# Dilated attention in an S5 hybrid layer: queries and values loaded a step ahead, V from three buffers, and the turned P kept in P's own tile

## The chip, the cores and the metric

The kernel runs on one core of a Trainium2 chip, in one launch. The metric is device time in microseconds (us), from one execution of the whole program. Before the change it is 2058.14 us, the median of three runs from 2056.48 to 2062.57. Engines are named as the profile names them: PE is the matrix engine (PEld its weight loads), DVE the vector engine, ACT the scalar engine, POOL GpSimd, and SP the engine that here only issues DMAs.

## The reference

One encoder layer on 2048 tokens of width 1024. An S5 state-space branch (32 groups of 16 channels, both directions) and an attention branch read the same normalised input; each is gated and projected, the two are mixed by sigmoid gates, and an output projection is added to the input.

```python
h = rms_norm(x, norm_w); proj = h @ w_in
u_a, z_a, q, k, v, z_b, g = split(proj)
for p, (window, dilation) in enumerate(((128, 1), (512, 4), (2048, 16))):
    o, lse = dilated_band_attention(q[:, :, p], k, v, window, dilation)   # 8 heads of 64
    # s = q k^T / 8, masked to the band; p = exp(s - max); o = (p v) / sum(p); lse = max + log(sum)
attn = sum over p of softmax(lse)[p] * o[p]
y_b = (attn * silu(z_b)) @ w_proj_attn
y_s = gelu(bidir_s5(u_a, ...));  a, b = split(y_s @ w_glu + b_glu)
y_a = (a * sigmoid(b) * silu(z_a)) @ w_proj_ssm
out = x + (sigmoid(g_a) * y_a + sigmoid(g_b) * y_b) @ w_out
```

Everything is float32. The kernel keeps that by splitting an operand into a high and a low part and taking three matmuls for one (`mm3`).

## The kernel before

The program has three phases. Phase A (to about 1083 us of the profiled span) makes the projections and the state-space part, and leaves Q, K and V in HBM. Phase B (to about 1670) is the attention. Phase C is the two branch projections, the mix and the output projection.

**Attention.** `attn_steps` lists 80 steps: four pairs of heads (hp), in each of them the three patterns in the order p = 1, 0, 2, in each of them four quarters of the queries (quad). A quarter with p 1 or 0 is two steps of two query tiles, with p 2 one step of four. The steps that share a quarter are a group, of which there are 48. A step j has three parts, and they are written one step apart: in turn i of the loop stand the scores of step i, the turning of step i-1 and the values of step i-2.

- `attn_scores`: in the first step of a group it issues the loads of q (two tiles, pool `qa`, two buffers) and v (one tile of five 128-row pieces, pool `vp`, two buffers). PE then multiplies q by K into two PSUM tiles `s` (of three); DVE's reduction (L1010) adds the mask, finds the row minimum and writes the masked scores to P in SBUF; ACT takes the exponential in place (L1014). P is two pairs of tiles `p00, p10` and `p01, p11`, one pair a step in turn.
- `attn_turn`: PE transposes the eight 128x128 blocks of P into two PSUM tiles `pp`; ACT (L1030) and DVE (L1032) each copy one of them to SBUF tiles `t0` and `t1`, which have two buffers each.
- `attn_values`: PE multiplies T by v into `po`, and at the end of a group it is copied out.

POOL issues the loads of q and v, but for the first two groups, which SP issues. With p = 1 the five pieces of v are five DMAs (L978): two edges of 64 rows, whose other half POOL sets to zero, and three whole pieces.

**Side work.** After each part, `self.run` lets PE do a share of other work: the remaining projections, the gated linear unit (`glu`), and the first part of the branch projection (`mix_early`). In `glu`, four results `fth` a block of tokens are made by ACT (L1189) and DVE (L1190, L1191) and stored to ACTA by SP (L1192); the next block's input is prepared in two halves `ft` (L1151 to L1156). `fth` and `ft` share two buffers of one pool (`ev`, tag e1), so the second half of `ft` waits until the store of the `fth` before it has landed. Matmuls of the side work write `acc`, of which there are two. `attn_merge` joins the three patterns of a quarter on POOL and DVE, through loads `ab` of weights that were stored to AL a moment before.

**What sets the order.** The program is written in the order of the loop, and is then put in order by the tile framework's scheduler (`schedule_with_timeline_sim=True`). That gives each engine one fixed list of instructions with semaphore waits. On the chip an engine works through its list in order; an instruction that waits holds everything behind it on the same engine.

Of the kernel before, what the change touches and what calls it, by code (L numbers as in the profile page):

```python
# [9 lines left out]
F32 = mybir.dt.float32  # L10
F32R = mybir.dt.float32r
# [14 lines left out]
def f(ap):  # L26
    return ap.bitcast(F32)


def at(t, off, dims):  # L30

    return bass.AP(tensor=t.tensor, offset=t.offset + off, ap=dims)
# [7 lines left out]
class Kern:  # L40
# [862 lines left out]
    def attn_setup(self, base, ctx, pctx):  # L903
        ap, R = self.pool, dict(ctx=ctx, side="right")
        self.op = ap("op", ctx=base, side="right")
        self.kp = ap("kp", **R)
        self.qa = ap("qa", bufs=2, **R)
        self.vp = ap("vp", bufs=2, **R)
        self.aw = ap("aw", bufs=2, **R)
        mp = ap("mk", **R)  # L910
        self.mg = ap("mg", **R)

        self.kh = [self.kp.tile([128, 2048], F32R, name=f"kh{h}") for h in range(2)]
        self.kl = [self.kp.tile([128, 2048], F32R, name=f"kl{h}") for h in range(2)]
        self.mk = {}
        for n in ("m2", "m1", "m3"):
            t = mp.tile(list(self.ins[n].shape), F32, name=n)
            self.nc.sync.dma_start(t, self.ins[n])
            self.mk[n] = t
        self.pS = ap("pS", bufs=3, space=PSUM, ctx=pctx)  # L920
        self.pT = ap("pT", bufs=2, space=PSUM, ctx=pctx)
        self.pO = ap("pO", bufs=1, space=PSUM, ctx=pctx)
        self.ev_ = 0
        self.P = [[self.aw.tile([128, 512], F32, name=f"p{h}{i}", bufs=1) for h in range(2)] for i in range(2)]
        for t in self.P[0] + self.P[1]:
            self.nc.vector.memset(t, 0.0)
        self.turn_ = 0
        self.O = [self.op.tile([128, 2048], F32, name=f"o{p}", tag=f"o{p}") for p in range(2)] + [None]

# [8 lines left out]
    def attn_steps(self):  # L938
# [12 lines left out]
            prev = x["group"]  # L951
        return out

    def attn_scores(self, x):
        nc, mm, R, C = self.nc, self.mm, 2048, 512
        hp, p, quad, per, g = x["hp"], x["p"], x["quad"], x["per"], x["group"]
        tiles = self.tiles[p]
        if x["sub"] == 0:
            late = hp > 0 or p != 1 or quad > 1

            g["q"] = [self.qa.tile([128, 512], F32R, name=f"q{h}") for h in range(2)]
            for h in range(2):
                o = (8 * p + 2 * hp + h) * 2 * 64 * R + 512 * quad
                (nc.gpsimd if late else nc.sync).dma_start(f(g["q"][h]), at(self.QT, o, [[R, 128], [1, 512]]))

            v = g["v"] = self.vp.tile([128, 5, 128], F32, name="v")
            c0 = 128 * hp
            if p == 2:
                (nc.gpsimd if late else nc.sync).dma_start(v[:, :4], at(self.V, 512 * quad * C + c0, [[4 * C, 128], [C, 4], [1, 128]]))
            else:  # L970
                run = 8 if p == 0 else 32
                base, m0 = (0, 4 * quad) if p == 0 else (512 * quad, 0)
                for m in range(m0, m0 + 5):
                    j0, j1 = max(run * m - run // 2, 0), min(run * m + run // 2, 128)
                    if j1 - j0 < run:
                        nc.gpsimd.memset(v[64:, m - m0], 0.0)
                    rows = [[512 * C, 4], [C, 4 * (j1 - j0)]] if p == 0 else [[C, 4 * (j1 - j0)]]
                    (nc.gpsimd if late else nc.sync).dma_start(v[:(16 if p == 0 else 4) * (j1 - j0), m - m0],  # L978
                                                               at(self.V, (base + 4 * j0) * C + c0, rows + [[1, 128]]))
            if p == 2:  # L980
                self.st[2] = self.aw.tile([128, 2, 2, 4], F32, name="st2", bufs=3)
            elif quad == 0:
                self.st[p] = self.aw.tile([128, 2, 2, 16], F32, name="st")
        q, kh, kl = g["q"], self.kh, self.kl
        st = x["st"] = self.st[p]
        w = 512 // per
        S = [self.pS.tile([128, per, w], F32, name="s") for h in range(2)]
        self.turn_ += 1
        x["P"] = [t.rearrange("p (i w) -> p i w", i=per) for t in self.P[self.turn_ % 2]]
        for i, t in enumerate(x["idx"]):  # L990
            qs = slice(128 * (t % 4), 128 * (t % 4) + 128)
            for h in range(2):
# [6 lines left out]
        for h in range(2):  # L999
            for i, t in enumerate(x["idx"]):  # L1000
                nk, mask = tiles[t][2], self.mk[tiles[t][1]]
                c = (t, 4 * (t % 4) + t // 4, t % 4)[p]
                least, o = st[:, 0, h, c:c + 1], 0
# [13 lines left out]
    def attn_turn(self, x):  # L1017

        nc, tiles = self.nc, self.tiles[x["p"]]
        x["blocks"] = blocks = [(i, b, b * tiles[t][3][0][1], vt, n) for i, t in enumerate(x["idx"])  # L1020
                                for b, (vt, n) in enumerate(tiles[t][3])]
        x["T"] = []
        for h in range(2):
            pp = self.pT.tile([128, 4, 128], F32, name="pp")
            for c, (i, b, o, vt, n) in enumerate(blocks):
                self.tr(pp[:, c], x["P"][h][:, i, o:o + 128], self.ident)
            ts = self.aw.tile([128, 4, 128], F32, name=f"t{h}")
            self.ev_ += 1
            if self.ev_ % 2:
                nc.scalar.activation(ts, pp, AF.Copy)  # L1030
            else:
                nc.vector.tensor_copy(ts, pp)  # L1032
            x["T"].append(ts)

    def attn_values(self, x):
        nc, mm, R = self.nc, self.mm, 2048
# [261 lines left out]
    def phase_b(self, base):  # L1298
        ctx, pctx = ExitStack(), ExitStack()
        self.attn_setup(base, ctx, pctx)  # L1300
        self.tiles = [self.q_tiles(p) for p in range(3)]
        self.st = [None] * 3
        steps = self.attn_steps()
        n = len(steps)
        self.beside, self.credit, self.since = self.fill(), 0.0, 0.0
        for r in range(4):
            self.k_load(0, r)
        self.run(LEAD)
        self.merges = []
        for i in range(n + 2):  # L1310
            self.merges = [m for m in self.merges if next(m, self) is not self]
            for d, fn in enumerate((self.attn_scores, self.attn_turn, self.attn_values)):
                j = i - d
                if 0 <= j < n:
                    x = steps[j]
                    fn(x)
                    if d == 0 and x["p"] == 2 and x["hp"] < 3:
                        self.k_load(x["hp"] + 1, x["quad"])
                    self.run(PACE[self.part] * (P2 if steps[min(i, n - 1)]["p"] == 2 else 1.0))
        if self.part == 2:  # L1320
            self.marks = {}
        for _ in range(4):
            self.run(TAIL)
            self.merges = [m for m in self.merges if next(m, self) is not self]
        pctx.close()
        ctx.close()
        self.run(1e9)
        self.flush()
# [169 lines left out]
```

## Time and profile before

| | |
|---|---|
| median of three runs | 2058.14 us |
| the profiled execution | 2057.8 us, its span 2056.0 us |
| PE busy, over the span | 1960.6 us (95%) |
| DVE, POOL, ACT busy | 1283.1, 838.7, 722.2 us |
| mean granted clock of PE | 0.978 of full speed |
| DMA engines' time for POOL's queue (q, v and K loads), for SP's | 8.2%, 42.3% |

The profile is of one execution. The 1.8 us between its time and its span lie outside what the instructions show. A busy share says how long an engine worked, not whether its work decided the end; for that one reads which waits PE has, and where.

### The profile page before, as it was taken

How to read it: one execution, taken by the hardware profiler on the slowest of the kernel's cores; microseconds unless marked ns; L12 is line 12 of the kernel's file. 1: busy time of each engine (PE TensorE's matmuls, PEld its weight loads, DVE VectorE, ACT ScalarE, POOL GpSimd, SP SyncE). 2: the span in 40 equal slices, each digit the busy share in tenths (PEclk: the TensorE clock that was granted, in tenths of full speed). 3: DMA queues.
4: the chain of work that ended last, by engine and by line, in shares of the span. 5: the costliest groups of instructions: out<-in, count | busy, mean ns of one | idle time of the engine just before them, and what ended most of it. 6: DMA issues, size and time to landing. Idle time of an engine off the chain costs nothing.

```text
span 2056.0 us, 37526 instructions
## 1 busy us (share of the span) xinstructions
PE 1960.6 (95%) x13612; PEld 1762.9 (86%) x13612; DVE 1283.1 (62%) x3276; ACT 722.2 (35%) x1789; POOL 838.7 (41%) x1128
## 2 busy tenths in 40 slices
PE   6899999999999999899998999999998978999999
PEld 6788899999787889899987878878887978899997
DVE  8867584878657688577765445456677656333332
ACT  4221242333222233233325545445665623101110
POOL 4410465548645755375543347457355232000000
PEclk9999999999999999999999999999999989999999
DMA  6632465346533454634465476567777447433332
GB/s 195 196 99 74 129 194 150 111 122 172 166 113 109 132 174 123 183 111 134 132 210 167 130 207 179 176 179 209 232 186 202 133 144 238 133 118 114 113 113 77
DMA packets 272059, 312.55 MB, mean 152 GB/s; under 512 B 86594, under 2 KB 182226, under 8 KB 271874
## 3 DMA queue, kind: packets, MB, share of 16 engines
q1 hardware_dynamic: 250914, 260.39, 42.3%
q0 software_dynamic: 20960, 49.76, 8.2%
q8 instruction: 108, 1.77, 0.4%
q14 instruction: 77, 0.63, 0.1%
HBM read 202.12 MB, written 105.71 MB: 150 GB/s over the span
## 4 chain that ended last, share of the span: by engine, by line
PE 62%; DVE 15%; DMA 12%; SPq 3%; POOL 3%; issue 3%; ACT 2%; DVEq 0%; POOLq 0%; ACTq 0%
PE acc L53 42%; PE po L53 11%; PE s L53 3%; PE pp L56 3%; DVE wlo L311 2%; DMA ab<-AL 2%; DMA raw<-in_w_in 1%; DMA ACTA<-fth 1%; DMA raw<-in_w_out 1%; PE y L53 1%; DMA AL<-e 1%; DVE zs L843 1%; DMA ST<-sr 1%; PE tp L56 1%; DVE zs L841 1%
## 5 line engine op out<-in xcount | busy, mean ns | idle before, releaser
L53 PE MATMUL acc<-xh,whi 128*128 128x512 f32 (+1 forms) x960 | 376.4, 393 | 18.1 <-DVE xsc L379 8.7
L53 PE MATMUL acc<-whi,xh 128*128 128x256 f32 x1280 | 368.3, 288 | 4.6 <-ACT qr L451 3.6
L53 PE MATMUL acc<-xl,whi 128*128 128x512 f32 (+1 forms) x960 | 366.5, 382 | 1.1 <-DVE xl L208 1.1
L53 PE MATMUL acc<-xh,wlo 128*128 128x512 f32 (+1 forms) x960 | 365.1, 381 | 0.0
L53 PE MATMUL acc<-whi,xl 128*128 128x256 f32 x1280 | 364.5, 285 | 0.4 <-POOL xl L263 0.4
L53 PE MATMUL acc<-wlo,xh 128*128 128x256 f32 x1280 | 364.6, 285 | 0.0
L53 PEld LDWEIGHTS acc<-whi,xh 128*128 128x128 f32 x1280 | 247.7, 194 | 7.7 <-ACT qr L451 4.2
L53 PEld LDWEIGHTS acc<-whi,xl 128*128 128x128 f32 x1280 | 247.7, 194 | 0.8 <-POOL xl L263 0.6
L53 PEld LDWEIGHTS acc<-wlo,xh 128*128 128x128 f32 x1280 | 248.0, 194 | 0.0
L53 PEld LDWEIGHTS acc<-xh,whi 128*128 128x128 f32 x960 | 184.3, 192 | 55.1 <-issue 12.0
L1014 ACT ACTIVATE p<-p,st 128x256 f32<-128x256 f32 (+2 forms) x384 | 173.2, 454 | 141.7 <-DVE st L1010 140.2
L311 DVE TENSOR_TENSOR wlo<-raw,whi 128x512 fp32r<-128x512 f32 x168 | 149.2, 906 | 107.2 <-ACT whi L310 106.4
L53 PEld LDWEIGHTS acc<-xh,wlo 128*128 128x128 f32 x960 | 183.7, 192 | 33.9 <-issue 0.4
L53 PEld LDWEIGHTS acc<-xl,whi 128*128 128x128 f32 x960 | 184.4, 192 | 28.9 <-DVE xl L208 1.5
L310 ACT ACTIVATE whi<-raw 128x512 fp32r<-128x512 f32 x176 | 102.9, 627 | 166.5 <-DMA raw<-in_w_in 141.5
L1010 DVE CUSTOM_DVE_ANT_0 p<-s,m 128x256 f32<-128x256 f32 (+2 forms) x376 | 116.1, 358 | 67.1 <-PE s L53 54.4
L53 PE MATMUL s<-kh,q 128*128 128x256 f32 (+3 forms) x400 | 105.4, 301 | 15.5 <-DVE st L1010 8.6
L53 PE MATMUL acc<-pair,wsh 128*128 128x256 f32 x512 | 100.1, 297 | 15.3 <-DVE cm L1372 10.7
L978 POOL DMA_DIRECT2D v<-V x150 | 92.6, 622 | 33.5 <-PE po L53 16.7
L53 PE MATMUL s<-kl,q 128*128 128x256 f32 (+3 forms) x400 | 103.1, 297 | 0.0
L56 PE MATMUL pp<-c_ident,p 128*128 128x128 f32 x640 | 92.8, 279 | 10.7 <-DVE t L1032 5.0
L53 PEld LDWEIGHTS acc<-pair,wsh 128*128 128x128 f32 x512 | 86.0, 205 | 17.3 <-issue 6.4
(333 smaller groups left out, 4383.3 us busy)
## 6 DMA issues: line engine op xcount, KB each, us to landing
raw<-in_w_in SPq DMA_DIRECT2D x176, 256.0 KB
q<-QT POOLq DMA_DIRECT2D x92, 256.0 KB, 4.2
ab<-AL SPq DMA_DIRECT2D x96, 128.0 KB
ug<-U SPq DMA_DIRECT2D x128, 64.0 KB
GA<-th SPq DMA_DIRECT2D x32, 256.0 KB
GB<-th SPq DMA_DIRECT2D x32, 256.0 KB
raw<-GB SPq DMA_DIRECT2D x32, 256.0 KB
xres<-in_x SPq DMA_DIRECT2D x32, 256.0 KB
```

What stands on the lines that cost most here:

```text
L53: return self.nc.tensor.matmul(*a, **k)
L56: return self.nc.tensor.transpose(*a)
L310: self.nc.scalar.activation(hi, t, AF.Copy)
L311: (eng or self.nc.vector).tensor_sub(lo, t, f(hi))
L841: V.tensor_tensor_scan(zs[:64, n, 2:258], r[:64].to_broadcast([64, 256]), z[:64, n], 0.0, op0=OP.mult, op1=OP.add)
L843: V.tensor_tensor_scan(zs[64:, n, 0:256][:, ::-1], r[64:].to_broadcast([64, 256]), z[64:, n, ::-1], 0.0, op0=OP.mult, op1=OP.add)
L978: (nc.gpsimd if late else nc.sync).dma_start(v[:(16 if p == 0 else 4) * (j1 - j0), m - m0], at(self.V, (base + 4 * j0) * C + c0, rows + [[ ...
L1010: self.marks["dve"] = nc.vector.tensor_tensor_reduce(pt, sc, mk, op0=OP.add, op1=OP.min, scale=-0.125, scalar=least if o else 3e38, accum_ ...
L1014: self.marks["act"] = nc.scalar.activation(pt, pt, AF.Exp, bias=st[:, 0, h, c:c + 1], scale=-1.0, accum_out=st[:, 1, h, c:c + 1])
```

## The change

Four things are done. The loads of q and v move into a function of their own, `attn_load`, called for step 0 ahead of the loop and for step i+1 ahead of the scores of step i. The pool of v has three buffers in place of two. With p = 1 the three whole pieces of v come in one DMA, so that a group has three DMAs in place of five. P is three pairs of tiles in place of two, with two more memsets at the start, and the transposed blocks are copied back from PSUM into the same pair of P, in place of a tile of their own.

```diff
-        self.vp = ap("vp", bufs=2, **R)
+        self.vp = ap("vp", bufs=3, **R)
...
-        self.P = [[self.aw.tile([128, 512], F32, name=f"p{h}{i}", bufs=1) for h in range(2)] for i in range(2)]
-        for t in self.P[0] + self.P[1]:
-            self.nc.vector.memset(t, 0.0)
+        self.P = [[self.aw.tile([128, 512], F32, name=f"p{h}{i}", bufs=1) for h in range(2)] for i in range(3)]
+        for p in self.P:
+            for t in p:
+                self.nc.vector.memset(t, 0.0)
...
+    def attn_load(self, x):
+        nc, R, C = self.nc, 2048, 512
+        hp, p, quad, g = x["hp"], x["p"], x["quad"], x["group"]
+        if x["sub"]:
+            return
+        late = hp > 0 or p != 1 or quad > 1
...
+            if p == 1:
+                (nc.gpsimd if late else nc.sync).dma_start(v[:, 1:4], at(self.V, (base + 64) * C + c0, [[C, 128], [128 * C, 3], [1, 128]]))
+            for m in range(m0, m0 + 5) if p == 0 else (0, 4):
...
-        x["P"] = [t.rearrange("p (i w) -> p i w", i=per) for t in self.P[self.turn_ % 2]]
+        x["P"] = [t.rearrange("p (i w) -> p i w", i=per) for t in self.P[self.turn_ % 3]]
+        x["T"] = [t.rearrange("p (b n) -> p b n", b=4) for t in self.P[self.turn_ % 3]]
...
-            ts = self.aw.tile([128, 4, 128], F32, name=f"t{h}")
+            ts = x["T"][h]
...
+        self.attn_load(steps[0])
         for i in range(n + 2):
             self.merges = [m for m in self.merges if next(m, self) is not self]
+            if i + 1 < n:
+                self.attn_load(steps[i + 1])
```

The rest of `attn_load` is the code that stood in `attn_scores`. Since the written program changes, so does the order that the scheduler gives each engine. On PE, DVE and SP it is the same as before from step 7 to step 58 of the attention (apart from the tiles' names), and in the tail after the attention; it differs in steps 2 to 7, in steps 59 to 76, and at the start of phase C. Three places follow. Line numbers shift by 8 to 11 from before to after: the reductions L1010 become L1020, the copies L1030 and L1032 become L1039 and L1041, `ft` L1152 to L1156 become L1160 to L1164, `fth` L1191 becomes L1199.

The first is DVE in steps 69 and 70, with `p_12520` and `p_12521` the P of step 70 before; this is before:

```order
2679 L1191 SCALAR_TENSOR_TENSOR fth<-acc,c_bglu,fth 128x256
2680 L1152 SCALAR_TENSOR_TENSOR ft<-ft,yz 128x512
2681 L1032 COPY t_18566<-pp 128x512
2682 L1010 ISA p_12519,st<-s,m_12505 128x256
...
2686 L1154 SCALAR_TENSOR_TENSOR ft<-ft,yz 128x512
2687 L1152 SCALAR_TENSOR_TENSOR ft<-ft,yz 128x512
2688 L311 TENSOR_TENSOR wsl<-raw,wsh 128x512
2689 L1156 SCALAR_TENSOR_TENSOR pair<-ft,pair 128x512
2690 L311 TENSOR_TENSOR wsl<-raw,wsh 128x512
2691 L1010 ISA p_12520,st<-s,m_12505 128x256
```

And this is DVE in the same steps after, where `p_12522` is the P of step 70 and the first row is the last reduction of step 69:

```order
2685 L1020 ISA p_12521,st<-s,m_12505 128x256
2686 L1020 ISA st 128x1
2687 L1199 SCALAR_TENSOR_TENSOR fth<-acc,c_bglu,fth 128x256
2688 L311 TENSOR_TENSOR wsl<-raw,wsh 128x512
2689 L1160 SCALAR_TENSOR_TENSOR ft<-ft,yz 128x512
2690 L1041 COPY p_12519<-pp 128x512
...
2693 L1160 SCALAR_TENSOR_TENSOR ft<-ft,yz 128x512
2694 L1078 COPY sr<-pp 64x128
2695 L1198 SCALAR_TENSOR_TENSOR fth<-fth,yz 128x256
2696 L1020 ISA p_12522,st<-s,m_12505 128x256
2697 L1020 ISA st 128x1
2698 L1199 SCALAR_TENSOR_TENSOR fth<-acc,c_bglu,fth 128x256
```

Between the second L1152 (after: L1160) and the first reduction of step 70 stood two cuts of a weight and a `pair`; now a small copy and one half of the next `fth` stand there.

The second is PE in the same steps, from the end of the 24 matmuls that make the first `fth` of the fence above; `pp` is turning, `s` scores, `po` values, `acc<-pair` the side work of `glu` (24 matmuls for one `fth`). This is before, and the row 8901 stands in the half of the scores of step 71 that needs a score tile from step 70:

```order
8846 L56 MATMUL pp<-c_ident,p_12518 128x128 x4
8847 L56 MATMUL pp<-c_ident,p_12519 128x128 x3
8848 L53 MATMUL acc<-pair,wgh 128x256 x2
...
8864 L56 MATMUL pp<-c_ident,p_12519 128x128
8865 L53 MATMUL s<-kh_12500,q_18508 128x256
...
8891 L56 MATMUL pp<-c_ident,p_12521 128x128 x4
8892 L53 MATMUL s<-kl_12501,q_18711 128x256
...
8901 L53 MATMUL s<-kh_12500,q_18712 128x256
8907 L53 MATMUL acc<-pair,wgh 128x256 x2
```

This is after, from the end of the 24 matmuls of the same `fth` to those of the fourth one (row 8920), which need the `acc` tile of the second; `p_12520` and `p_12521` at its start are those of step 66, `p_12522` and `p_12523` those of step 67:

```order
8854 L53 MATMUL po<-p_12520,v 64x128
8855 L53 MATMUL po<-p_12521,v 64x128
...
8862 L53 MATMUL s<-kl_12502,q_18263 128x256
8863 L53 MATMUL acc<-pair,wgh 128x256 x2
...
8881 L53 MATMUL po<-p_12522,v 64x128
8882 L53 MATMUL acc<-pair,wgh 128x256 x2
...
8904 L53 MATMUL po<-p_12523,v 64x128
8905 L56 MATMUL pp<-c_ident,st 64x128
...
8919 L56 MATMUL pp<-c_ident,p_12521 128x128 x4
8920 L53 MATMUL acc<-pair,wgh 128x256 x2
```

Before, 48 matmuls of side work, 16 of turning and 16 of scores stand between the first `fth` and the scores of step 71 that need step 70's tile. After, 48 of side work, 16 of turning, 13 of scores and the 16 of the values of steps 66 and 67 stand between it and the fourth `fth`; those values stood behind the whole stretch before.

The third is SP at the start of phase C, where the sixteen pieces of `w_out` are loaded (`in_w_out`); before:

```order
705 L1110 DMA ab<-AL 64x512 x6
706 L302 DMA raw<-in_w_out 128x512 x3
707 L1345 DMA pair<-ACTA 128x1024
708 L1359 DMA raw<-GB 128x2x256
709 L302 DMA raw<-in_w_out 128x512 x2
...
723 L302 DMA raw<-in_w_out 128x512
724 L1345 DMA pair<-ACTA 128x1024
725 L1359 DMA raw<-GB 128x2x256
726 L1421 DMA out<-xres 128x512
```

After:

```order
705 L1118 DMA ab<-AL 64x512 x6
706 L302 DMA raw<-in_w_out 128x512
707 L1370 DMA raw<-GB 128x2x256
708 L1370 DMA raw<-GA 128x2x256
709 L1130 DMA ACTB<-ab 128x512
...
724 L302 DMA raw<-in_w_out 128x512 x2
725 L1432 DMA out<-xres 128x512
726 L302 DMA raw<-in_w_out 128x512
727 L1426 DMA xres<-in_x 128x512
728 L302 DMA raw<-in_w_out 128x512
```

Behind the loads `ab` three pieces of `w_out` stood together and now one does, and the last two pieces stand behind the first store of the output.

## Rows read from the trace of the kernel before

**Rows 1.** Windows: stretch, length, busy time (instructions) by engine, PE's clock, DMA share, GB/s.

```profile
1104.00:1525.00 421.00, 413.57 (x3093) 346.03 (x3091) 232.98 (x897) 228.73 (x760) 208.37 (x325) 1.00 0.63 182
1230.90:1237.00 6.10, 6.10 (x47) 5.20 (x49) 3.08 (x15) 3.68 (x14) 0.70 (x1) 1.00 0.23 53
1528.00:1538.00 10.00, 9.94 (x73) 8.42 (x73) 8.25 (x31) 7.82 (x24) 9.66 (x16) 0.70 0.71 181
1560.00:1568.40 8.40, 0.40 (x4) 0.19 (x2) 4.68 (x9) 4.53 (x11) 3.05 (x3) 0.78 0.50 155
1568.40:1575.00 6.60, 6.43 (x29) 6.17 (x30) 5.37 (x12) 2.71 (x10) 3.69 (x4) 0.51 0.75 235
```

**Rows 2.** Waits of PE, 1100 to 1670 us: waiting <- released by, us, times, longest.

```profile
PE s L53 <- DVE st L1010: 8.6, 2, 8.0
...
PE pp L56 <- ACT t L1030: 2.7, 1, 2.7
```

**Rows 3.** Waits of PE, 1080 to 1100 us.

```profile
PE s L53 <- DMA v<-V: 6.7, 1, 6.7
```

**Rows 4.** POOL's loads of v: durations in ns, least, median, most.

```profile
L978 POOL DMA_DIRECT2D v<-V x150: 537/666/883, 1107.7 to 1603.4; - x150
```

**Rows 5.** PE's timeline: start, us, instruction; values of steps 28, 66, 68.

```profile
1284.38 1.09 PE L53 MATMUL po<-t,v 128*64 128x128 f32 x14
...
1575.56 1.74 PE L53 MATMUL po<-t,v 128*64 128x128 f32 x26
...
1587.07 1.09 PE L53 MATMUL po<-t,v 128*64 128x128 f32 x16
```

**Rows 6.** DVE's timeline: first reductions of steps 31, 69, 71.

```profile
1287.13 0.42 DVE L1010 CUSTOM_DVE_ANT_0 p<-s,m 128x256 f32<-128x256 f32 x1 [1.95 <-PE s L53]
...
1552.02 0.42 DVE L1010 CUSTOM_DVE_ANT_0 p<-s,m 128x256 f32<-128x256 f32 x1
...
1584.36 0.42 DVE L1010 CUSTOM_DVE_ANT_0 p<-s,m 128x256 f32<-128x256 f32 x1
```

**Rows 7.** PE's timeline: a short wait, and around the longest in phase B.

```profile
1230.82 0.66 PE L56 MATMUL pp<-c_ident,p 128*128 128x128 f32 x4 [1.90 <-DVE sr L1084]
...
1550.71 0.28 PE L53 MATMUL acc<-pair,wgl 128*128 128x256 f32 x1
...
1568.40 0.58 PE L53 MATMUL s<-kh,q 128*128 128x256 f32 x1 [8.00 <-DVE st L1010]
```

**Rows 8.** The chain of waits to that point: start, us, what.

```profile
1555.30 0.50 DVE fth L1191
...
1555.82 7.22 DMA ACTA<-fth
...
1563.06 0.64 ACT ft L1151
...
1567.66 0.33 DVE p L1010
```

**Rows 9.** DVE's timeline: two operations of the chain, each short and long.

```profile
1545.56 0.41 DVE L1190 SCALAR_TENSOR_TENSOR fth<-fth,yz 128x256 f32<-128x256 f32 x1
...
1553.72 1.54 DVE L1190 SCALAR_TENSOR_TENSOR fth<-fth,yz 128x256 f32<-128x256 f32 x1
...
1555.70 0.68 DVE L1152 SCALAR_TENSOR_TENSOR ft<-ft,yz 128x512 f32<-128x512 f32 x1
...
1563.72 2.13 DVE L1152 SCALAR_TENSOR_TENSOR ft<-ft,yz 128x512 f32<-128x512 f32 x1 [5.45 <-ACT ft L1151]
```

**Rows 10.** The chain of waits, 1440 to 1510 us: three stores of `fth`.

```profile
1470.19 5.81 DMA ACTA<-fth
...
1495.14 5.30 DMA ACTA<-fth
...
1504.95 3.20 DMA ACTA<-fth
```

**Rows 11.** PE's timeline: its wait for the last piece of `w_out`.

```profile
1750.12 0.72 PE L53 MATMUL po<-woh,mh 128*128 128x512 f32 x2 [1.55 <-ACT woh L310]
```

More of the change, by code (lines that the diff above doesn't have):

```diff
@@ L952, in attn_steps @@
         return out
+    def attn_load(self, x):
[4 more added lines that the diff above has]
+        late = hp > 0 or p != 1 or quad > 1
+        g["q"] = [self.qa.tile([128, 512], F32R, name=f"q{h}") for h in range(2)]
+        for h in range(2):
+            o = (8 * p + 2 * hp + h) * 2 * 64 * R + 512 * quad
+            (nc.gpsimd if late else nc.sync).dma_start(f(g["q"][h]), at(self.QT, o, [[R, 128], [1, 512]]))
+        v = g["v"] = self.vp.tile([128, 5, 128], F32, name="v")
+        c0 = 128 * hp
+        if p == 2:
+            (nc.gpsimd if late else nc.sync).dma_start(v[:, :4], at(self.V, 512 * quad * C + c0, [[4 * C, 128], [C, 4], [1, 128]]))
+        else:
+            run = 8 if p == 0 else 32
+            base, m0 = (0, 4 * quad) if p == 0 else (512 * quad, 0)
+            if p == 1:
+                (nc.gpsimd if late else nc.sync).dma_start(v[:, 1:4], at(self.V, (base + 64) * C + c0, [[C, 128], [128 * C, 3], [1, 128]]))
+            for m in range(m0, m0 + 5) if p == 0 else (0, 4):
+                j0, j1 = max(run * m - run // 2, 0), min(run * m + run // 2, 128)
+                if j1 - j0 < run:
+                    nc.gpsimd.memset(v[64:, m - m0], 0.0)
+                rows = [[512 * C, 4], [C, 4 * (j1 - j0)]] if p == 0 else [[C, 4 * (j1 - j0)]]
+                (nc.gpsimd if late else nc.sync).dma_start(v[:(16 if p == 0 else 4) * (j1 - j0), m - m0],
+                                                           at(self.V, (base + 4 * j0) * C + c0, rows + [[1, 128]]))
     def attn_scores(self, x):
-        nc, mm, R, C = self.nc, self.mm, 2048, 512
+        nc, mm = self.nc, self.mm
         hp, p, quad, per, g = x["hp"], x["p"], x["quad"], x["per"], x["group"]
@@ L958, in attn_scores @@
         if x["sub"] == 0:
[L959 to L979, printed above, removed]
             if p == 2:
@@ L1021, in attn_turn @@
                                 for b, (vt, n) in enumerate(tiles[t][3])]
-        x["T"] = []
         for h in range(2):
@@ L1032, in attn_turn @@
                 nc.vector.tensor_copy(ts, pp)
-            x["T"].append(ts)
     def attn_values(self, x):
```

## The prediction

> **What bounds the kernel now.** I read the stretches of the span first, then PE's waits, then the chain behind the longest of them, and at last DVE's and PE's timelines there.
>
> Over the long middle of the attention, 1104 to 1525 us, PE is busy 413.57 of 421.00 us at full clock [rows 1]. Nothing that makes another engine quicker can save more than the difference there. What is left in phase B is in its last third: from 1560.00 to 1568.40 PE works 0.40 us, and in the 6.60 us behind it its clock is 0.51 of full speed, which is the lower of its two levels (1.2 in place of 2.4 GHz); from 1528 to 1538 the mean is 0.70, a mixture of the two [rows 1].
>
> PE's waits between 1100 and 1670 us say who is late: DVE's reductions with 8.0 us at once, and an ACT copy of a turned P with 2.7 [rows 2]. In the whole answer of that view no DMA of q or v is named. The only wait for a load of the attention is the first, 6.7 us at the start [rows 3]. So earlier loads, a third buffer and fewer DMAs have nothing to take off PE's path between start and end; if the change is to tell, it is by the order that it makes.
>
> The chain to the 8.0 us says what they hang on [rows 8]. DVE finishes the first `fth` of a block at 1555.80, SP stores it, and 7.22 us pass until it has landed. Only then may ACT write the second half of `ft` into that buffer (1563.06). DVE's part of `ft` is next in DVE's list, and behind it stand two weight cuts, a `pair`, and only then the reductions of step 70 (1567.66), which PE's scores of step 71 need for a free score tile.
>
> **The change part by part.** The sum is made against the profiled execution, 2057.8 us (span 2056.0, 1.8 outside it); it is 0.34 below the median of the runs.
>
> *The start.* Both memsets more run on DVE while PE waits for the first v [rows 3]; SP's first loads stand in the same order, so this wait stays. Steps 2 to 7 get a new order around it. 0 us, bounds -2 to +2 (a wait of [rows 7]'s short kind, 1.90, more or fewer).
>
> *Loads.* With p = 1 two of five DMAs of v go in 16 groups, of which POOL issues 14: 28 issues at 0.67 us, some 19 us of POOL's time, if the DMA of three pieces is issued as fast as one of them [rows 4], and none if it takes as long as three. Either way PE waits for no v, so 0 on the path. Loads of q stand in POOL's list near the same `ab` operations as before, one group earlier at most; q's wait is bounded by 0 and the same 1.90. I take 0.
>
> *The turned P in P's tile, and the ring of three.* The copies are the same in number and size. What is new is a wait: the reductions of step j+3 write the pair that the values of step j read, so DVE must wait for PE's values of step j. Behind a waiting reduction stands everything else on DVE's list. In the steady part this costs nothing: values of step 28 end at 1284.38 + 1.09 = 1285.47, reductions of step 31 begin at 1287.13, with 1.66 us to spare [rows 5, 6]; of the 52 steps from 7 to 58, 51 have between 1.6 and 8.4. In the last third it was otherwise: values of step 66 began at 1575.56, but step 69's reductions at 1552.02; those of step 68 ended at 1588.16, step 71's reductions had begun at 1584.36 [rows 5, 6]. There the order must change, and does: nine steps, 64 to 72, were so before.
>
> *The 8.0 us.* In the order after, the values of steps 66 and 67 stand ahead of the place where PE ran dry, and DVE reaches `fth` by another way. How much PE has to do from the end of the first 24 matmuls to its wait: before, 1568.40 - 8.00 - (1550.71 + 0.28) = 9.41 us [rows 7]. After, the same without three scores (47 matmuls in 6.10 us, 0.13 each [rows 1], so -0.39) and with two steps of values (1.09 each [rows 5], +2.18): 11.2 us. There stand the matmuls of the fourth `fth`, which need the `acc` of the second, and DVE frees that one only behind the second half of `ft`. How long DVE needs to there, from the same start:
>
> - first `fth` done: before at 1555.80, 4.81 us after the start. One operation of it, L1190, took 1.54 us where 0.41 is its usual time [rows 9]; without this 3.68. I take the middle, 4.25.
> - the store: 7.22 here, and 3.20, 5.30 and 5.81 at three of its kind earlier [rows 8, 10]. I take 5.30.
> - ACT's half 0.64 [rows 8]; DVE's L1152 0.68, or 2.13 as here [rows 9]. I take 0.68.
> - then a small copy, L1198, one reduction and L1199: about 0.42, 0.41, 0.42 and 0.50, 1.75 together [rows 6, 8, 9] (for the copy I take a reduction's time).
>
> Together 12.62, so PE waits 1.4 us in place of 8.0: -6.6. By the low ends of all lines it is 9.95 and PE doesn't wait (-8.0); by the high ends 16.55, and PE waits 5.35 (-2.65). What is late next is the same engine, with the second `fth`.
>
> *The clock behind it.* Before, 6.43 us of work ran at 0.51 [rows 1], of which 6.43 x 0.49 = 3.15 us are lost. After a wait of 1.90 us at 1230.82 the clock was 1.00 [rows 1, 7]; after that of 2.7 it was at the mixture of 0.70. A wait of 1.4 is nearer to the first: -3.15, bounds -3.15 and 0.
>
> *The earlier wait of 2.7.* In the order after, one copy stands ahead of the `ft` that held it, but two exponentials of step 63 still stand behind that `ft`. I take 0; bounds -2.7 with 9.94 x 0.30 = 2.98 us of clock [rows 1, 2], and +2.7.
>
> *The pieces of `w_out`.* The last two are issued behind the first output store. Before, PE waited 1.55 us for the last piece [rows 11]. After, PE's list has both token halves of the first column half mixed with the second column half, so that the late pieces are also used later. I take 0; it can save the 1.55, or cost one landing as slow as the slowest store here, 7.2.
>
> The sum: 2057.8 - 6.6 - 3.15 = 2048.05, so **2048 us**. Its own range is 2046 (no wait left) to 2053 (a wait of 3 us or so, and the clock falls).
>
> **The rivals.**
>
> *The store takes as long as before.* If the store again lands after 7.22, and DVE's two operations are long again, PE waits 5.35 and its clock falls behind it: 2057.8 - 2.65 = 2055.2. For it speaks that the store is issued amid loads of weights in both orders; against it that three stores of the kind took 2 to 4 us less [rows 8, 10]. The DMA engines were at half their capacity in the stretch of the wait and at 0.75 behind it [rows 1], so a store that shares them is at least possible. The Trainium skill, "DMA: Bandwidth & Descriptors", Issuing engines are not separate DMA queues, says that DMAs of all issuing engines run on the same 16 DMA engines and interleave. By that rule loads of q and v that POOL issues a group earlier are one more thing for the store to share with; it would bring this rival's time, not the forecast's. No row here shows a store with and without such a load beside it.
>
> *The new wait decides (slower).* Place: DVE in steps 64 to 72, where the values were later than the ring now allows. Price: step 68's values would hold step 71's reductions by 1588.16 - 1584.36 = 3.8 us [rows 5, 6]. It decides from the point at which PE's fill between the two is used up, so that the wait on DVE becomes one on PE. Two such steps give 2057.8 + 7.6 = 2065.4 with the old wait of 8.0 kept in another place. For it speaks that nine steps in a row were so; against it that PE's order after puts the values ahead, and PE loses nothing by doing the same matmuls in another order.
>
> *Both waits go.* If the new order also loses the 2.7: 8.0 + 3.15 + 2.7 + 2.98 = 16.8 less, 2041.0. Against it stand the two exponentials behind `ft`.
>
> **How the numbers follow.** Forecast 0.38, store as slow as before 0.31, new wait 0.19, both waits gone 0.12. A measurement of this kernel can tell about 0.3% from no change, 6.2 us, so faster is below 2052.0 and slower above 2064.3. Faster takes most of the forecast (0.33), all of both gone (0.12) and a little of the slow store: 0.46. Slower takes most of the new wait: 0.17. The rest is 0.37. The range 2039 to 2065 holds all but the far part of the two outer cases.
>
> **What would show it.** PE's order is as told, so the profile after must have no wait of PE for DVE L1020 or `acc` over 3 us between 1540 and 1600, full clock behind it, and values of steps 66 and 67 ahead of it. DMA issues of v on POOL fall by 28 with PE's waits unchanged. Step j+3's reductions must wait for step j's values in no step from 7 to 58. A PE wait for q or v, a wait of over 2 us in steps 60 to 76 that ends with the values, or one of over 2 us for `woh` would make the sum wrong; so would a change of time from 1104 to 1500 us.

## The result and the profile after

The kernel after took 2073.84 us (median of 6 runs, 2068.61 to 2079.36) and the kernel before 2058.02 us (6 runs) on the same chip: a ratio of 1.0074, interval 1.0056 to 1.0091. It is slower, by some 15.8 us. The forecast was 2048 with a range from 2039 to 2065, so both were wrong.

One statement ahead of the prediction is wrong too, and it matters. DVE's and SP's orders are not the same from step 7 to step 58. The scheduler moved the work of the merges there: DVE's product `ab` (L1119 before, L1127 after), the small operations `mn` and `e` ahead of it, and SP's loads of `ab`. For PE the statement nearly holds, and that was not enough.

The windows of [rows 1], read from the kernel after (the columns are the same):

```profile
1104.00:1525.00 421.00, 400.07 (x2946) 331.72 (x2945) 224.69 (x861) 222.31 (x742) 190.00 (x291) 0.99 0.61 177
...
1528.00:1538.00 10.00, 8.39 (x81) 7.98 (x80) 4.87 (x26) 4.40 (x13) 3.39 (x4) 1.00 0.60 161
1560.00:1568.40 8.40, 8.40 (x74) 7.67 (x73) 6.36 (x18) 6.29 (x19) 8.32 (x12) 0.82 0.81 188
1568.40:1575.00 6.60, 2.95 (x20) 2.71 (x19) 4.83 (x16) 1.31 (x6) 2.57 (x3) 0.87 0.47 119
```

In the stretch that I had called full, 1104 to 1525, PE works 400.07 us in place of 413.57. The hole at 1560 is filled, another stands at 1568.40 (2.95 of 6.60 us), and the kernel is slower. PE's waits from 1100 to 1670 us, to be held against [rows 2] (waiting, released by, us in total, times, longest):

```profile
PE pp L56 <- DVE p L1041: 14.9, 6, 3.8
PE acc L53 <- DVE fth L1199: 5.7, 3, 2.4
PE po L53 <- issue: 3.1, 1, 3.1
PE po L53 <- ACT o L1066: 3.1, 3, 1.6
PE pp L56 <- DVE sr L1092: 2.9, 5, 0.9
...
PE s L53 <- DVE st L1020: 1.0, 1, 1.0
```

The one long wait is gone, and six for DVE's copies of the turned P have come; before, those copies had three, 5.0 us in all. Why those copies are late is in DVE's own waits from 1100 to 1500 us. Before:

```profile
DVE ab L1119 <- DMA ab<-AL: 22.8, 8, 7.4
```

After:

```profile
DVE ab L1127 <- DMA ab<-AL: 39.3, 8, 8.7
```

The same eight products wait 39.3 us in place of 22.8 for the loads of their weights. Part of that only changes its name: DVE's waits for the loads `s`, which stand ahead in each merge, fall from 18.6 to 11.0 us. DVE's timeline shows two of the products at close hand (start, us, instruction, shape, idle time before it and what ended it). The second product before:

```profile
1247.55 1.07 DVE L1119 TENSOR_TENSOR ab<-ab,o 128x512 f32<-128x512 f32 x1 [3.31 <-DMA ab<-AL]
```

and the second and third after, with what stands around them:

```profile
1236.30 0.69 DVE L1041 COPY p<-pp 128x512 f32<-128x512 f32 x1 [0.99 <-PE pp L56]
1245.65 0.69 DVE L1127 TENSOR_TENSOR ab<-ab,o 128x512 f32<-128x512 f32 x1 [8.66 <-DMA ab<-AL]
1246.26 0.68 DVE L1066 COPY o<-po 128x512 f32<-128x512 f32 x1
1246.86 0.91 DVE L1103 TENSOR_TENSOR mn<-s 128x8 f32<-128x8 f32 x1
...
1261.45 0.69 DVE L1127 TENSOR_TENSOR ab<-ab,o 128x512 f32<-128x512 f32 x1 [6.47 <-DMA ab<-AL]
1262.06 0.68 DVE L1041 COPY p<-pp 128x512 f32<-128x512 f32 x1
```

The load of the second product ended within 2 us of the same time in both kernels (1247.55 and 1245.65, each released by it). DVE came to it at 1236.99 after (1245.65 - 8.66) and at 1244.24 before (1247.55 - 3.31), so it stood waiting 7 us earlier. Behind it stand a copy of `po` and, at the third product, a copy of the turned P. PE's timeline answers there:

```profile
1247.05 1.09 PE L53 MATMUL po<-p,v 128*64 128x128 f32 x16 [3.12 <-issue]
...
1262.80 1.11 PE L56 MATMUL pp<-c_ident,p 128*128 128x128 f32 x4 [2.65 <-DVE p L1041]
```

For the first the view names no releaser; PE starts 0.11 us after the copy of `po` has ended on DVE. Two more waits of `po`, 1.58 us at 1397.74 and 2.17 at 1429.92, are put down to POOL, but there too a copy of `po` on DVE ended 0.10 us before PE started. The wait at 1262.80 is released by the copy that stood behind the third product. The chain of waits over 1234 to 1263 us goes the same way (start, us, what):

```profile
1239.81 5.72 DMA ab<-AL
...
1245.65 0.14 DVE ab L1127
1245.79 0.47 issue
1246.26 0.68 DVE o L1066
...
1254.83 6.50 DMA ab<-AL
...
1261.45 0.10 DVE ab L1127
...
1262.06 0.69 DVE p L1041
1262.75 0.04 issue
1262.80 0.47 PE pp L56
```

In the order of DVE's list one can count how early each product comes: the number of reductions that stand ahead of it, for the first twelve of the sixteen merges.

| kernel | first third | second third | last third |
|---|---|---|---|
| before | 108, 120, 132, 142 | 208, 220, 228, 242 | 312, 321, 346, 346 |
| after | 108, 116, 124, 132 | 208, 216, 224, 232 | 312, 320, 332, 346 |

So in the first two thirds the products come up to ten reductions earlier, and in the last one of them comes fourteen earlier. Around the second one the two lists read thus, before:

```
L1010 ISA p_12521,st<-s,m_12503 128x256
L1010 ISA st 128x1
L1032 COPY t_14643<-pp 128x512
L1119 TENSOR_TENSOR ab<-ab,o_12526 128x512
L393 TENSOR_SCALAR th<-th 128x512
L1010 ISA p_12518,st<-s,m_12503 128x256
```

and after:

```
L1020 ISA p_12519,st<-s,m_12503 128x192
L1020 ISA st 128x1
L1041 COPY p_12523<-pp 128x512
L1127 TENSOR_TENSOR ab<-ab,o_12530 128x512
L1066 COPY o_12531<-po 128x4x4x32
L1103 TENSOR_TENSOR mn<-s_14386 128x8
```

To say in which stretch the time went I compare the start of the same matmul, counted from PE's first (PE's list is nearly the same), in the two profiled executions. The difference grows by 8.3 us in what was 1224 to 1284 of the kernel before, by 7.6 in 1371 to 1456, by 3.9 in 1501 to 1585, and by 1.5 us net everywhere else, together 21.3 (this execution was the slowest of the six; its span is 2077.6 us). The first two stretches hold merges of the first and the second third.

### The profile page after: what moved, and what is told of

Same layout as the page of the kernel before. It is cut to its first block, busy times and chain, and to the rows that moved or that the text cites. A ratio compares the mean times of both kernels' runs of the same rounds, so it can differ in the third digit from the quotient of the medians.

```text
span 2077.6 us, 37540 instructions
## 1 busy us (share of the span) xinstructions
PE 1961.7 (94%) x13612; PEld 1761.7 (85%) x13612; DVE 1296.0 (62%) x3278; ACT 722.7 (35%) x1789; POOL 824.1 (40%) x1100
## 4 chain that ended last, share of the span: by engine, by line
PE 58%; DMA 14%; DVE 14%; SPq 4%; issue 4%; POOL 3%; ACT 2%; DVEq 0%; ACTq 0%; POOLq 0%
PE acc L53 40%; PE po L53 10%; PE s L53 3%; DMA ab<-AL 2%; PE pp L56 2%; DMA raw<-in_w_in 2%; DVE wlo L311 2%; DMA AL<-e 1%; SPq L1118 1%; DMA s<-ST 1%; PE y L53 1%; DMA ST<-sr 1%; DMA raw<-in_w_out 1%; DMA ACTA<-fth 1%; PE tp L56 1%
## 5 line engine op out<-in xcount | busy, mean ns | idle before, releaser
L1020 DVE CUSTOM_DVE_ANT_0 p<-s,m 128x256 f32<-128x256 f32 (+2 forms) x376 | 116.0, 358 | 60.5 <-PE s L53 57.7
L53 PE MATMUL acc<-pair,wgh 128*128 128x256 f32 x512 | 99.6, 293 | 6.5 <-DVE fth L1199 5.7
L53 PE MATMUL po<-p,v 128*64 128x128 f32 x1280 | 95.7, 283 | 10.0 <-issue 3.1
L56 PEld LDWEIGHTS pp<-c_ident,p 128*128 128x128 f32 x640 | 74.3, 142 | 33.7 <-DVE p L1041 11.2
```

Of the source, the lines that this page charges most:

```text
L53: return self.nc.tensor.matmul(*a, **k)
L56: return self.nc.tensor.transpose(*a)
L1020: self.marks["dve"] = nc.vector.tensor_tensor_reduce(pt, sc, mk, op0=OP.add, op1=OP.min, scale=-0.125, scalar=least if o else 3e38, accum_ ...
```

## The experiments

Each ran five rounds beside the kernel before on its chip; a ratio is to that, with its interval. "Stretches" are the growths just described, against the profiled execution of before, for 1224 to 1284, 1371 to 1456, 1501 to 1585 and 1585 to 1653.

| kernel | us | ratio, interval | stretches | DVE's waits for `ab` loads, 1100 to 1500 |
|---|---|---|---|---|
| after | 2073.84 | 1.0074, 1.0056 to 1.0091 | 8.3, 7.6, 3.9, -1.2 | 39.3 |
| v3_alone | 2067.72 | 1.0043, 1.0026 to 1.0060 | 5.1, 5.9, -1.1, -1.0 | 41.5 |
| ring_alone | 2057.13 | 0.9990, 0.9978 to 1.0003 | -0.5, 0.2, -6.0, 6.0 | 17.7 |
| ahead_alone | 2059.32 | 1.0007, 0.9993 to 1.0020 | -1.5, -0.2, 0.0, 0.8 | 21.0 |
| no_v3 | 2060.81 | 1.0011, 0.9996 to 1.0026 | 0.3, 1.8, 2.3, -0.5 | 24.5 |
| ab_on_pool | 2065.40 | 1.0034, 1.0021 to 1.0046 | 8.5, 0.5, -0.1, 0.8 | none |
| all_padded | 2067.25 | 1.0042, 1.0024 to 1.0059 | -0.6, 1.0, 2.0, 4.6 | 25.7 |
| q_on_act | 2064.91 | 1.0040, 1.0021 to 1.0058 | 5.3, 4.4, -1.1, -0.3 | 36.1 |
| ring_ft | 2055.13 | 0.9987, 0.9972 to 1.0002 | -0.9, 0.2, -3.3, 3.3 | 18.6 |
| v3_padded | 2059.53 | 1.0003, 0.9989 to 1.0018 | -0.1, -0.4, 4.1, -2.0 | 21.9 |
| padded_but_last | 2060.90 | 1.0012, 0.9994 to 1.0029 | 0.1, 0.1, 5.5, -0.5 | 25.0 |

In the first two stretches the kernels that can't be told from before show -1.5 to 1.8, so that more than that is an effect there. In the last two such kernels show -6.0 to 6.0, and what one loses the next often gives back; these two are read only with the medians. A profile is of one execution: those of v3_alone, all_padded and q_on_act were the fastest of their runs, 4.1 to 4.4 us below the median, so their stretches add up to less than the median lost; that of ab_on_pool was the slowest of ten.

**Which of the four edits: v3_alone.** The kernel before, with the three whole pieces of V in one DMA and nothing else.

```diff
-                for m in range(m0, m0 + 5):
+                if p == 1:
+                    (nc.gpsimd if late else nc.sync).dma_start(v[:, 1:4], at(self.V, (base + 64) * C + c0, [[C, 128], [128 * C, 3], [1, 128]]))
+                for m in range(m0, m0 + 5) if p == 0 else (0, 4):
```

> The kernel before with one edit: with p = 1 the three whole pieces of v come in one DMA. Order theory (the slowdown is DVE's place for the merge's product ab, which stands 4 to 10 reductions earlier in DVE's list and waits there for its load, because this edit shortens POOL's list): the product stands after 116, 124 and 132 reductions as in the changed kernel, PE waits some 15 us more between 1220 and 1430 than before, and the time is 2066 to 2074 us. Ring theory (the new wait of the reductions for the values costs the time): the time is that of before, 2058 within 6. Traffic theory (earlier or larger loads make the loads of ab land later): slower, with loads of ab that take 2 us or more longer from issue to landing than before.

This edit by itself loses 8.1 us of the 15.8 (2067.72 against 2059.58 on that chip). DVE's products stand almost as early as after (108, 116, 124, 132; 208, 216, 224, 231), and the products at 1256 and 1268 of its DVE timeline wait 6.15 and 4.01 us, where the same two waited 2.63 and 0.73 before:

```profile
1241.74 0.69 DVE L1121 TENSOR_TENSOR ab<-ab,o 128x512 f32<-128x512 f32 x1 [6.14 <-DMA ab<-AL]
1256.47 0.69 DVE L1121 TENSOR_TENSOR ab<-ab,o 128x512 f32<-128x512 f32 x1 [6.15 <-DMA ab<-AL]
1268.53 0.69 DVE L1121 TENSOR_TENSOR ab<-ab,o 128x512 f32<-128x512 f32 x1 [4.01 <-DMA ab<-AL]
```

It loses at the same matmuls as the kernel after, among them those that before runs at 1254.66, 1397.47 and 1399.32. PE's waits from 1220 to 1430 us sum to 16.0 in place of 6.2, so 9.8 more and not the 15 expected. The traffic theory can be read from it too. From SP's issue of the last `ab` load of a merge to the product that it releases, the products that waited over 1 us (1200 to 1440) took 4.2 us on average before, 4.9 after, 5.0 in v3_alone and 5.1 in v3_padded, a kernel further down that isn't slower: at most 0.9 later, and not the 2 that this theory needs.

**The other edits: ring_alone, ahead_alone and no_v3.** ring_alone is the kernel before with three pairs of P and the turned blocks kept in them. ahead_alone is the kernel before with `attn_load` called a step ahead, with two V buffers. no_v3 is the kernel after with five DMAs of V again:

```diff
-            if p == 1:
-                (nc.gpsimd if late else nc.sync).dma_start(v[:, 1:4], at(self.V, (base + 64) * C + c0, [[C, 128], [128 * C, 3], [1, 128]]))
-            for m in range(m0, m0 + 5) if p == 0 else (0, 4):
+            for m in range(m0, m0 + 5):
```

> The kernel before with one edit: P is three pairs and the turned P goes back into its own pair. Order theory: the product ab stands where it stood before but for one of 16 places, so the time is 2058 within 6 us; the 8.0 us wait may move, worth up to 11. Ring theory: slower by 8 to 16, 2066 to 2074. Traffic theory: 2058 within 6.

> The kernel before with the loads of q and v a step ahead and nothing else (two buffers of v, five DMAs, two pairs of P and T in its own tiles). Order theory: the product ab stands in the same 16 places as before, and the time is 2058 within 6 us. Traffic theory (early loads make the loads of ab land later): slower, 2066 to 2074.

> The changed kernel with five DMAs for v with p = 1, as before; loads a step ahead, three V buffers and the ring of three stay. Order theory: the product ab stands in the places of before, PE's extra waits between 1220 and 1430 are gone, and the time is 2050 to 2062 us. Ring theory: still slow, 2068 to 2076. Traffic theory: still slow, since the loads are still a step ahead, 2068 to 2076.

None of the three can be told from before. So the ring, the earlier loads and the third buffer cost nothing measurable, as the prediction had it, and without the DMA of three pieces the rest of the change is worth nothing either. The third buffer was run only together with the ring and the earlier loads.

**Where it waits: ab_on_pool.** The kernel after, with the first product of a merge on POOL.

```diff
-            V.tensor_mul(ab[0], ab[0], self.O[0][:, c])
+            G.tensor_mul(ab[0], ab[0], self.O[0][:, c])
```

> The changed kernel with the merge's product ab * O[0] on POOL in place of DVE, 16 operations of 1.3 us. Order theory: DVE's 39 us of waits for ab are gone, PE's waits for turned P and values between 1220 and 1430 with them, and the time is 2056 to 2066 us. Ring theory and traffic theory: the wait is only named otherwise, 2070 to 2078 us.

At 2065.40 it is at the upper edge of what was expected, so about half of the loss is gone. DVE has no wait for `ab` left, but PE's waits in 1200 to 1440 us are not gone:

```profile
PE pp L56 <- DVE p L1041: 6.7, 3, 3.8
PE po L53 <- DVE o L1066: 5.3, 1, 5.3
```

In 1371 to 1456 the loss went. In 1224 to 1284 the growth of 8.5 us is of another kind: 5.4 of it come at the one wait of 5.3, and no merge holds DVE there. DVE stands 6.30 us for a cut of a weight, for which ACT waited 6.63 us for its load (`raw<-in_w_in`), and the copy of `po` stands behind it:

```profile
1273.85 3.48 DVE L311 TENSOR_TENSOR wlo<-raw,whi 128x512 fp32r<-128x512 f32 x1 [6.30 <-ACT whi L310]
1277.26 0.68 DVE L1066 COPY o<-po 128x512 f32<-128x512 f32 x1
```

Another 1.4 come at 1244.17, where a copy of a turned P stands behind the merge's `mn`, which waited 5.01 us for its loads `s`. So with the product off DVE most of what it held is gone from both stretches; why the weight came late in this kernel was not looked at.

**Transfer or order: all_padded, v3_padded, padded_but_last and q_on_act.** A DMA of 192 KB could also cost by itself. To keep it and still have the old order, two one-row DMAs (each brings a row that is there already) stand behind it, so that POOL's list again holds five issues a group:

```diff
+                for m in (2, 3):
+                    (nc.gpsimd if late else nc.sync).dma_start(v[:1, m], at(self.V, (base + 64 + 128 * (m - 1)) * C + c0, [[C, 1], [1, 128]]))
```

> The changed kernel, and behind the DMA of three pieces two more DMAs of one row each of the same data, so that POOL has five DMAs a group again. The product ab stands nearly where it stood before (108, 120, 128, 142, 208, 220, 228, 242 reductions ahead of it). Order theory: PE's extra waits between 1220 and 1430 are gone and the time is 2055 to 2064 us. DMA theory (the one large DMA itself costs, by what it moves or when): they stay, 2068 to 2076.

The time missed what was expected: 2067.25. The mechanism did not. The products stand at 108, 120, 128, 142 and 208, 220, 228, 242, nearly as before; the two stretches that had lost 15.9 us together lose 0.4; PE's waits from 1200 to 1440 us sum to 8.0 (after 19.8, before 6.7). Most of what was left in its trace lay in 1501 to 1653 (6.6 us), in the last third, where the products stand at 312, 324, 338, 344, an order of its own. PE's timeline of all_padded shows two waits there, the first of the kind of [rows 7]:

```profile
1565.78 0.55 PE L53 MATMUL s<-kh,q 128*128 128x256 f32 x1 [6.66 <-DVE st L1022]
...
1595.47 0.77 PE L53 MATMUL acc<-pair,wgh 128*128 128x256 f32 x2 [5.13 <-DVE fth L1201]
```

Two more kernels put that to the test. v3_padded is the same padding on the kernel before, where the last third then stands as before (312, 322, 346, 346). padded_but_last is all_padded with the five plain DMAs of V for the last pair of heads (`if p == 1 and hp < 3`), where it stands as in no_v3 (312, 328, 336, 346).

> The kernel before with the load of three tiles of V in one transfer, and behind it two one-row loads that bring the same values again, so that the queue of GpSimd holds as many issues as in the kernel before. VectorE's merge products stand after 108, 120, 128, 142 and 208, 220, 228, 242 reductions, nearly as before (before 108, 120, 132, 142, then the same), the last third as before (312, 322, 346, 346). Theory 1 (the order of VectorE's list costs the time, the large transfer itself nothing): 2056 to 2061 us, the same as before within 0.3 per cent, waits of VectorE for the merge's loads near 23 us, waits of PE from 1200 to 1440 us near 8. Theory 2 (the transfer of 192 KB as such costs): near v3_alone's 2067.7, and PE's waits in that stretch near 17.

> The changed kernel with the two one-row loads behind the large load of V (as in all_padded), but for the last pair of heads, where the five single loads of the kernel before stand. VectorE's merge products in the last third then stand as in no_v3 (312, 328, 336, 346) and not as in all_padded (312, 324, 338, 344). Theory 1 (what all_padded still lost, 8 us, lay in the order of the last third): 2057 to 2062 us, and the stretches that the kernel before runs from 1501 to 1653 us within 3 us of no_v3's. Theory 2 (it came from the large transfers or from the added loads themselves): near all_padded's 2067.

Both times came out as the order has it and not as the transfer has it: 1.0003 against v3_alone's 1.0043 with the same large transfers, and 1.0012 against all_padded's 1.0042. The intervals of the first pair lie apart, those of the second just overlap. The stretches bear out less: padded_but_last still grows by 5.0 us from 1501 to 1653 in its profiled execution, over 3 more than no_v3, and gains a little elsewhere. DVE's waits for `ab` loads in v3_padded are near those of before, and PE's in 1200 to 1440 us are short in sum:

```profile
PE pp L56 <- DVE t L1036: 4.7, 3, 2.9
PE pp L56 <- DVE sr L1088: 2.8, 3, 1.4
```

q_on_act goes the other way: the kernel before, its V in five DMAs, only ACT issues the loads of q, so that POOL has less to issue without any large transfer.

```diff
-                (nc.gpsimd if late else nc.sync).dma_start(f(g["q"][h]), at(self.QT, o, [[R, 128], [1, 512]]))
+                (nc.scalar if late else nc.sync).dma_start(f(g["q"][h]), at(self.QT, o, [[R, 128], [1, 512]]))
```

> The kernel before with the loads of q issued by ACT in place of POOL; v still comes in five DMAs. The product ab stands early, as in the changed kernel (108, 116, 124, 132, 208, 216, 224, 232). Order theory: DVE waits some 35 to 40 us for ab between 1100 and 1500 (22.8 before), PE some 8 to 15 more, and the time is 2064 to 2074 us. DMA theory: nothing of the large DMA is in it, so 2052 to 2062.

Its products stand at 108, 116, 124, 132 and 208, 216, 224, 232, the places of after, and it is 1.0040, with 36.1 us of DVE's waits for `ab`. The stretch 1224 to 1284 loses 5.3. Of the 4.4 that 1371 to 1456 loses, 3.0 were gained just ahead of it, where PE's list has another order, so little is left there; 4.1 more go from 1456 to 1501, with a wait of PE for ACT behind a store of `fth`, which isn't a merge's. PE's waits from 1200 to 1440 us are 11.5 in all, 4.8 more than before, and not the 8 to 15 expected. So it bears out the order in the time and in the first third only. That it also gives ACT more to issue is a second change that this kernel can't be freed of.

**What the 8.0 us hung on: ring_ft.** ring_alone, with `ft` in two buffers of its own, so that it doesn't wait for the store of `fth`.

```diff
-            t = self.ev.tile([128, 2, 256], F32, name="ft", tag="e1")
+            t = self.aw.tile([128, 2, 256], F32, name="ft", bufs=2)
```

> The kernel before with the ring of three pairs of P, and the SBUF that it gives back spent on ft: two buffers of its own, so that it shares none with fth and waits for no store. If the 8.0 us of before hang on that store, they and the lower clock behind them go: 8 to 12 us less than before, 2046 to 2052. If DVE's list is late there for other reasons, another wait takes the place: 2055 to 2062.

It gave some 3 us (0.9987), with an interval that reaches 1.0002, and at 2055.13 it is where it was expected if another wait takes the place. PE's waits from 1500 to 1660 us show that:

```profile
PE acc L53 <- DVE fth L1191: 7.9, 3, 4.1
PE pp L56 <- DVE sr L1070: 4.4, 1, 4.4
PE acc L53 <- DVE mn L1102: 2.5, 1, 2.5
```

The wait for a score tile is gone, and others take its place. But in ring_alone, where `ft` shares its buffers with `fth` as before, it is gone as well (the longest there is 2.0 us), at 0.9990. So whether the 8.0 us hung on the store is not shown by this run. What the two show is that taking that wait away is not worth its length: the last third gives back what one takes from it.

## Why the prediction was wrong, step by step

**"In the steady part this costs nothing", and the orders alike up to step 58.** This is the step that failed. I had compared PE's order and the ring's margins, and taken 0 for everything from 1104 to 1500 us; the text said itself that a change of time there would make the sum wrong. It was 15.9 us in two stretches of the profiled execution. Of the 31 us between the sum (2048.05) and that execution (2079.36), those are the half; nearly all of the rest is the term of the 8.0 us and its clock, below. The runs show the cause of the 15.9: the edit with the fewest words ("three whole pieces in one DMA") moved DVE's merge products ahead of reductions and copies that PE needs, while the loads they wait for did not come earlier by as much (for the second product 1.9 us, where DVE came 7.25 earlier). With the large DMA in place and the order undone, the two stretches lose at most 1.0 us each (v3_padded, all_padded, padded_but_last), and v3_padded has the time of before; an early order without that DMA is slower again (q_on_act), though its trace shows the merges' part in the first third only. That the scheduler moves the merges because it reckons POOL free sooner is what the edits have in common; its reckoning itself was not looked at. The padding also keeps POOL's own queue as long as before on the chip, so a part for POOL's speed, beside the order, is not excluded by it.

**Loads: 0.** Right as far as the path goes: no wait of PE for q or v in the attention but the first, 6.8 us as against 6.7 [rows 3]; the two that the view puts down to POOL end with DVE's copies of `po`, as said above. The saving on POOL was between its bounds: the three-piece DMA issues in 776 ns, a fifth more than the single one's 647 in the same run, and POOL's issues on these lines took 80.3 us in place of the 92.6 that L978 took before, 12.3 less and not 19. POOL's group rows after, to be held against [rows 4]:

```profile
L981 POOL DMA_DIRECT2D v<-V x108 | 69.4, 647 | 34.6 <-PE po L53 19.6 <-issue 9.6 <-PE s L53 5.2
L975 POOL DMA_DIRECT2D v<-V x14 | 10.9, 776 | 37.4 <-PE po L53 37.4
```

I used that saving to say that it couldn't help. I didn't ask what it would do to the order.

**The ring.** Right: its wait doesn't tell. DVE's reductions waited for PE's values 2.4 us in all between 1100 and 1670, and nothing from 1145 to 1500:

```profile
DVE p L1020 <- PE po L53: 2.4, 4, 1.1
```

The rival in which this wait decides gave the right sign and 7.6 of the 15.8 us, by a mechanism that isn't there.

**The 8.0 us and the clock.** The wait went, and the one that the sum put in its place, for the second `fth`, came where it was forecast and with its size: 1.39 us for 1.4. That is luck, since both sides of it were off. DVE was done with that `fth` at 1594.25, 15.2 us after the end of the first 24 matmuls (1579.07) and not 12.6; PE was busy or held up until 1593.01, 13.9 us and not 11.2, with two waits of 0.88 and 0.73 among them. PE's timeline has it last; the waits ahead of it are what the sum put at nothing:

```profile
1536.96 1.10 PE L53 MATMUL po<-p,v 128*64 128x128 f32 x16 [1.61 <-ACT o L1066]
...
1540.91 0.50 PE L53 MATMUL acc<-pair,wgh 128*128 128x256 f32 x2 [1.89 <-DVE fth L1199]
...
1558.49 1.06 PE L56 MATMUL pp<-c_ident,p 128*128 128x128 f32 x8 [3.76 <-DVE p L1041]
...
1573.36 1.12 PE L56 MATMUL pp<-c_ident,p 128*128 128x128 f32 x4 [3.65 <-DVE p L1041]
...
1594.40 0.48 PE L53 MATMUL acc<-pair,wgh 128*128 128x256 f32 x2 [1.39 <-DVE fth L1199]
```

The third and the fourth are merges again: DVE stood at 1557.48 for `s` and at 1570.17 for `ab`.

```profile
1557.48 0.26 DVE L1103 TENSOR_TENSOR mn<-s 128x8 f32<-128x8 f32 x1 [2.99 <-DMA s<-ST]
...
1570.17 1.37 DVE L1127 TENSOR_TENSOR ab<-ab,o 128x512 f32<-128x512 f32 x1 [3.76 <-DMA ab<-AL]
```

All waits for `fth` together are 5.7 us. The clock was not given back either: it is a mixture of its two levels behind three of the waits, 0.77 after 2.65 us, 0.79 after 3.76 and 0.75 after 3.65 (windows after: stretch, length, busy times, clock, DMA share, GB/s):

```profile
1247.00:1253.00 6.00, 4.57 (x33) 3.49 (x34) 5.57 (x18) 3.25 (x11) 4.05 (x4) 1.00 0.39 107
1262.80:1269.80 7.00, 7.00 (x41) 5.64 (x42) 4.68 (x13) 3.60 (x11) 4.33 (x4) 0.77 0.62 163
1558.50:1566.50 8.00, 8.00 (x68) 7.22 (x68) 7.86 (x26) 6.80 (x23) 7.82 (x12) 0.79 0.64 146
1573.30:1580.00 6.70, 6.64 (x50) 6.36 (x50) 5.71 (x21) 3.44 (x11) 0.58 (x1) 0.75 0.61 159
```

Behind the last two that is 8.00 x 0.21 + 6.64 x 0.25 = 3.3 us lost, as much as the 3.15 of before. So the stretch of this wait, 1501 to 1585, grows by 3.9 us in place of shrinking by 9.75. In ring_alone the wait of 8.0 went too, and its time is that of before: the length of a wait was taken for its worth.

**The store as slow as before, and both waits gone.** The store of the first `fth` took 4.62 us (`ACTA<-fth` at 1585.37), below the 5.30 of the sum, so the rival of the slow store did not come; DVE's two operations behind it were long again (1.34 and 1.28 us). The wait of 2.7 did go: from 1528 to 1538 the clock is 1.00, though PE works only 8.39 us.

**`w_out`.** The longest wait for a piece is 1.09 in place of 1.55 [rows 11]. Waits for weights that DVE cuts (`raw` L1411) are 2.10 at 1740.97 and 0.95 at 1745.06, where one of 1.82 stood before. From 1670 of before to the end the difference grows by 1.2 us in this one execution; no experiment looked at it.

**What stays open.** v3_alone has 1.0043 and the whole change 1.0074 (their intervals just overlap), though the other edits can't be told from nothing without it. The orders of the first two thirds are nearly alike in the two, and the last third is not (v3_alone 312, 320, 340, 349). From 1501 to 1585 after loses 5.0 us more. That fits, but no run took the last third of after alone. Why all_padded loses what it does there is read from its trace; shown is only that plain DMAs for the last pair of heads bring its time back.

## What to carry to other kernels

Where a scheduler orders the program, compare the order of every engine over the whole stretch that you price at nothing, above all of small side work that waits for a DMA: one such instruction a few places earlier in an in-order list holds everything behind it. An edit that only takes issues off an engine that isn't the bottleneck can be the one that costs, so price it by what it moves. A long wait is worth its length only if nothing else is late behind it: read what stands next on every engine, not on one. And test a suspected cost by keeping the edit and restoring the order, as with the two one-row loads here: that tells the transfer from the shorter list of issues in one run.

## What the runs showed of the hardware

- One DMA of three pieces (128 x 3 x 128) issued from POOL in 776 ns (mean of 14), one of a single piece in 647 ns (mean of 108) in the same run.
- PE's clock stayed at 1.00 over the 6 us behind a wait of 3.12 us at 1247.05, and was a mixture, 0.77, over the 7 us behind a shorter one of 2.65 at 1262.80; ahead of the latter PE had waited 3.12 and 1.26 us in 16 us. The length of one wait doesn't tell what the clock does behind it.
- Phase A (to the first matmul of the scores) ran 3.3 us shorter to 3.7 us longer than before's in single profiled executions, though no edit touches it and PE's list there is the same. Single profiles can't place a difference of a few us there; the stretches above are differences within phase B.
